# Loads of the modulations' weights during the recurrence: issued by ScalarE on its own DMA queue instead of by SyncE on the common one

## The chip, the core and the metric

The kernel runs on one core of a Trainium2 chip. The metric is the device time of one execution in microseconds (us), lower is better. The engines are TensorE (PE in the profile; its weight loads are PEld), VectorE (DVE), ScalarE (ACT), GpSimd (POOL) and SyncE (SP), which only issues DMA transfers. SPq stands for SP's own instruction sequence.

## What is computed

Two layers of a diffusion backbone over 512 latent tokens (l) and 256 context tokens (c), width 1024, all in float32. Cut to what matters here:

```
def ada_mod(cond, w, b):                 # nine modulations of 1024 columns for each layer
    m = jax.nn.silu(cond) @ w + b        # w: 1024 x 9216
    return m.reshape(cond.shape[:-1] + (N_MOD, D_MODEL))

for li in range(DEPTH):                  # DEPTH = 2
    ml, mc = ada_mod(c, mod_w[li], mod_b[li]), ada_mod(c_ctx, mod_w[li], mod_b[li])
    xl, xc = first SwiGLU half-step (modulations 0 to 2)
    out = concat(fourier(f), window_attention(q, k, v), rwkv7(r, k, v, ...)) @ w_out   # modulations 3 to 5
    xl, xc = second SwiGLU half-step (modulations 6 to 8)
```

The RWKV-7 part is a bidirectional recurrence over the tokens with a 64x64 state for each of six heads.

## The kernel before, in words

The work runs layer by layer: feed-forward half, input projections of the mixer, the recurrence (`rwkv`), output projection, feed-forward half. Python code emits the instructions; a scheduler then sets the order on each engine from its own estimate of when operands are ready. Each engine, and SP too, then works through its own sequence strictly in order: an instruction that waits for a semaphore holds up everything behind it on that engine.

**The recurrence** is done in six groups of 256 tokens in each layer (two directions, three blocks of tokens), with products over chunks of 64 tokens. Group numbers run from 0 to 5; `d_0_4` in the rows of the order is the DRAM scratch of layer 0, group 4.

**`inverses` (lines 930 to 998)** inverts, for a group, the small triangles on the diagonal. It is the part that goes through DRAM, and it matters below. Its steps: products on PE, copied out by ACT (L961, tile LAB); masked on DVE (L969, L971); written to DRAM (L975, `d<-W`); read back in another layout (L976, `W<-d`); 62 short DVE instructions that do the elimination (L987 and L989, thirty-one pairs, of which the first L987 has the form 96x31); written to DRAM again (L992), read back (L993); put on the diagonal (L997). DVE stands still at its first L987 until L976 has landed, whatever else is behind it.

**Fill work.** Attention (L1083 to L1140), the modulations that are needed later (`mod_steps`, L239) and part of the output projection (`out_part`) are pumped into the recurrence (`pump`), a piece for each stretch of PE work. `mod_steps` makes modulations 5 to 8 of the layer and, in layer 0, also 0 to 4 of the next one. Half a modulation takes two loads of weights, each 128 x 4 x 512 (1 MB), into two buffers (`wmod`, L251), eight matmuls for each load (L256, tile `pf`, one PSUM buffer), a copy by ACT (L262, tile `macc`), a 2 KB load of the bias into it (L263), short matmuls (L266 or L271), and a copy of the result (L267 or L272). A load has to wait until PE has used the buffer's last content.

The line that the change touches, and its surroundings:

```
def part(q, cs=cs, st=st):
    w = wp.tile([128, 4, 512], F32, name="wmod", bufs=2)
    self.dma(w, self.a["mod_w"][l, q * 512:(q + 1) * 512, cs].rearrange("(k p) c -> p k c", p=128))   # L251
    if q == 0:
        st["ps"] = pf([128, 512])
    for g in range(4):
        r = slice(32 * g, 32 * g + 32)
        self.behind(nc.tensor.matmul(st["ps"][r], lhsT=self.cTz[:, 4 * q + g], rhs=w[:, g], ...))     # L256
```

`self.dma` is `nc.sync.dma_start`: before the change all transfers of the kernel are issued by SP, on one queue. Other loads that SP issues in the recurrence: the groups' operands (`AtB`, `BtB`, `KI` in L1285, `HB` in L1287, `W<-opd` in L954), the queries of a token tile (`q<-qd`, L1062), the values' rows (`Z`, L1321).

Of the kernel before, what the change touches and what calls it, by code (L numbers as in the profile page):

```python
# [32 lines left out]
# tiles of the feed-forward columns in the chunks after the first; buffers of gated products: raw (then low), high  # L33
# [5 lines left out]
class Halves:  # L39
    """Products of weights and tokens by Strassen's scheme (Winograd's form): the halves are of the  # L40
    inner dimension, of the tokens, and gates with values; 7 products of quarters instead of 8."""

    def __init__(self, net, n0, n):
        self.net, self.nc, self.w = net, net.nc, n // 2
        hi, lo = net.hT["h"], net.hT["o"]
        m = self.w
        q = lambda x, t, k: x[:, 4 * k:4 * k + 4, n0 + t * m:n0 + t * m + m]
        self.a = {f"a{t + 1}{k + 1}": (q(hi, t, k), q(lo, t, k)) for t in range(2) for k in range(2)}
        # the quarter a21 isn't needed by itself
        self.a["s3"] = self.a["a21"]  # L50

    def sums(self, anchor):
        """The second half of the work comes behind the anchor."""
# [31 lines left out]
    def weights(self, wi, c0):  # L85
        """The quarters of a tile of gates and one of values, and their sums."""
        nc, net = self.nc, self.net
# [12 lines left out]
    def unit(self, ws, sg, pool):  # L100
        """silu(gates) * values."""
# [42 lines left out]
# buffers of the ring of weights that stay through the mixers' projections, and more: raw, split  # L144
# [3 lines left out]
class Net:  # L148
# [78 lines left out]
    def behind(self, inst, anchor=None):  # L227
        """The engine of both issues inst after the anchor."""
# [10 lines left out]
    def mod_steps(self, l, m, wp, pf):  # L239
        """Steps for the modulation m of layer l: the sums by quarters of the array, then their sums with the bias."""  # L240
# [3 lines left out]
        for h in range(2):  # L244
# [3 lines left out]
            def part(q, cs=cs, st=st):  # L248
                self.mark('mod')
                w = wp.tile([128, 4, 512], F32, name="wmod", bufs=2)  # L250
                self.dma(w, self.a["mod_w"][l, q * 512:(q + 1) * 512, cs].rearrange("(k p) c -> p k c", p=128))  # L251
# [24 lines left out]
    def mod(self, l, ms, stg, rows):  # L276
        """The modulations ms (at most two) of layer l."""
# [34 lines left out]
    def norm_cols(self, l, n, m_shift, m_scale):  # L312
        """Columns of g*(1+scale) and of shift, by stream."""
# [8 lines left out]
    def gate_row(self, l, n, m, s, half):  # L322
        """The row half*m*g, on all partitions."""
# [11 lines left out]
    # The arena's tiles hold rows in turn (4), loaded rows (2), halves of transposes (2) and gate rows (2);  # L335
    # in the feed-forward halves the sums of quarters of the normed tokens
# [18 lines left out]
    # In the passage from one part to the next the engines keep to the order of the program  # L355
# [10 lines left out]
    def squares(self, x, junk):  # L366
        """The root of the mean of the squares."""
# [18 lines left out]
    def prenorm(self, t, x, cols, xn, junk):  # L386
        """Normalises the token tile t; every second one is transposed with the one before it. Two steps."""
# [11 lines left out]
    def flush(self, rest=True):  # L399
        """Emits the transposes that were put off, behind products that needn't wait for them."""  # L400
        for e in self.late:
            e[0] -= 1
        while self.late and (rest or self.late[0][0] == 0):
            self.some(4)
            self.late.pop(0)[1]()
        if rest:
            self.some(4)

    def some(self, n=1):
        """What follows the transposes, by quarters."""  # L410
# [39 lines left out]
    def residual(self, t, o, grow, xn, po):  # L450
        """x + norm(o)*grow for the token tile t, with o's halves as they come. Three steps."""
# [3 lines left out]
        for i in range(2):  # L455
            cs = slice(i * 512, i * 512 + 512)
            # of the halves' mean squares
# [11 lines left out]
    def passage(self, toks, outs, post):  # L469
        """The last products of the tokens, by halves (outs), and what follows them, a token behind."""  # L470
# [27 lines left out]
    def load_w(self, srcs, shape):  # L498
        """Loads weights (pieces by columns, or by rows of two dimensions)."""
# [11 lines left out]
    def turning(self, j, name, shape, dt):  # L511
        """The next tile of the ring, raw (0) or split (1)."""
# [9 lines left out]
    def cut(self, x, e=None):  # L522
        """Splits x, of at most 512 columns in all, exactly: (high, low), each of float32r."""
# [9 lines left out]
    def split_w(self, srcs, shape, e=(None, None)):  # L533
        """Weights, split exactly, by halves of their first free dimension."""
# [4 lines left out]
    def prod(self, ps, w, s, c0, n):  # L539
        """Sums in ps the products of the weights w with n tokens of stream s, from c0."""  # L540
# [13 lines left out]
    def ffn(self, l, wi, wo, toks, post, last, mods=(), early=None):  # L554
        """last: loads that follow the last chunk's products with the tokens."""
# [10 lines left out]
        # the last 64 columns come first: gates and values in one tile  # L566
# [12 lines left out]
        def split_g(sg, w):  # L579
            gh = fp.tile([128, NT], F32R, name="gh", bufs=GB)  # L580
            if w == 64:
                # the low parts below the high ones
# [10 lines left out]
        def gated(sg, cs, w, pg, pu):  # L593
            """silu(gates) * values; of a tile with both, on its upper half."""
# [9 lines left out]
        def first(ch):  # L604
            """The first chunk, by pairs of token tiles, as they become ready."""
# [81 lines left out]
    def early_keys(self, l, raw):  # L687
        """The context's keys of the recurrence, while the latent tokens are on their way."""
# [10 lines left out]
    def mixer(self, l, need_ctx):  # L699
# [5 lines left out]
        with self.pool("mixo", bufs=1) as mo, ExitStack() as outer:  # L705
# [8 lines left out]
            # partial output projections: of the Fourier heads, and of the attention heads as well  # L714
            self.part = [[self.dp.tile([128, D], F32, name=f"part{l}_{j}_{i}") for i in range(6)] for j in range(2)]
            # decays over the chunks
            pcs = mo.tile([128, 2, 3, 12], F32, name="pcs")
            self.rw = dict(pcs=pcs)
            # in DRAM: head sums times values; values in token-major; queries; by direction the recurrence's
            # unit keys by the decay so far, rates and keys by its inverse, receptances by the decay  # L720
# [6 lines left out]
            # keys' high parts, on both halves, by head; low parts  # L727
# [5 lines left out]
            with self.pool("inp", side="right") as rp, ExitStack() as inner:  # L733
# [5 lines left out]
                def load(c0):  # L739
                    """Columns c0 (a list of pieces) of the input projection's weights, split."""  # L740
                    return self.split_w([win[:, :, c:c + w] for c, w in (c0 if isinstance(c0, list) else [(c0, 128)])], [128, 8, 128])

                def proj(c0, ctxs=True, pcx=None):
                    """Columns c0 of the input projection: (latent, context) in PSUM."""
# [9 lines left out]
                # the recurrence's inputs; the context's first, while the latent tokens are on their way  # L754
                self.mark('inp')
                # rows 96 to 101: the heads' rows scaled by k_k
# [65 lines left out]
                # row 64: ones, and the decays' bias  # L822
# [23 lines left out]
                def operands(z):  # L846
                    """The recurrence's operands of direction z."""
# [11 lines left out]
                    for p in range(3):  # L859
# [11 lines left out]
                        # av: twice the in-context rate, less one  # L871
# [26 lines left out]
                for p in range(3):  # L898
                    r = rs[p]
                    v = conv(6 + p, kns[p], True)  # L900
                    # values, token-major
# [9 lines left out]
                    # the heads' sums of products of keys and receptances, times the values  # L911
# [10 lines left out]
    def diagonals(self, pool):  # L922
        """The recurrence's operands of two heads, on the blocks of a diagonal; KI: keys beside it, identities on it."""
# [13 lines left out]
    def triangles(self, pool):  # L937
        """Buffers of the inverses of the recurrence's triangles."""
# [4 lines left out]
    def inverses(self, gi, z, t0, psum, mm):  # L943
        """Of a group of 256 tokens from t0, direction z, the products of rates and unit keys, and the inverses of
        their 32x32 blocks on the diagonal."""
# [18 lines left out]
        # the blocks on the diagonal, of every unit a row of blocks; their inverses  # L964
# [7 lines left out]
        # of every block on one partition the even columns of the inverse, on another the odd ones  # L972
# [803 lines left out]
```

## Time and profile before

| | us |
|---|---|
| median of three runs | 3571.68 (3569.08 to 3574.14) |
| span of the profiled execution | 3573.4 |
| recurrence of layer 0, with the fill work | about 890 to 1340 |
| recurrence of layer 1, the part with loads of `wmod` | about 2710 to 2930 |
| busy over the span: PE, DVE, ACT, POOL | 3262.0, 2352.3, 1378.0, 809.4 |
| loads of `wmod` (L251) | 52, of 1 MB each |

The page gives the span of the profiled execution from its first to its last instruction and no other time of it. The span lies inside the spread of the three runs and 1.7 us above their median, so terms that are summed against it are brought to the median by taking 1.7 us off. A matmul counts as busy from its start to a modelled end; at the lower of TensorE's two clock levels the same matmul shows about twice the duration. "Releaser" is what ended a wait.

### The profile page before, as it was taken

The page shows a single profiled execution, that of the slowest core. Times are in us where ns is not written, and L with a number is a line of the kernel's source. Part 1 is how long each engine was busy: PE and PEld are TensorE (multiplying, and loading weights), DVE is VectorE, ACT ScalarE, POOL GpSimd, SP SyncE. Part 2 cuts the span into 40 slices and gives each one's busy share as a digit, 9 for nine tenths or more (in the row PEclk, how much of TensorE's full clock was granted, in tenths as well). Part 3 has the DMA queues.
Part 4 walks back from the last instruction along what each step waited for, and adds up shares of the span by engine and source line. Part 5 has one row for each costly group of instructions (what it writes and reads, how often), then busy time and mean ns, then how long its engine had stood idle before and what let it go on. Part 6 is the DMA issues. An engine that isn't in the chain of part 4 may idle for free. (4 is left out here: it accounts for less than half of the span.)

```text
span 3573.4 us, 51830 instructions
## 1 busy us (share of the span) xinstructions
PE 3262.0 (91%) x19801; PEld 2729.5 (76%) x19801; DVE 2352.3 (66%) x4374; ACT 1378.0 (39%) x2818; POOL 809.4 (23%) x609
## 2 busy tenths in 40 slices
PE   7999998998778897999998999998995898979998
PEld 5689997776556655899997899997774676758997
DVE  4577777456466656677777767777464666467897
ACT  3333335342334334433335433335342433344444
POOL 0222222023101013322222322222041000024333
PEclk9999999999889988999999999999997878779999
DMA  5432224245667556222224222224355563253333
GB/s 179 148 119 71 71 69 138 87 141 134 153 172 177 160 187 214 60 69 68 71 71 140 61 71 65 71 71 138 97 166 119 157 157 71 68 182 89 101 107 101
DMA packets 540346, 410.13 MB, mean 115 GB/s; under 512 B 210405, under 2 KB 462188, under 8 KB 540098
## 3 DMA queue, kind: packets, MB, share of 16 engines
q1 hardware_dynamic: 540098, 406.82, 39.4%
q8 instruction: 156, 2.56, 0.3%
q14 instruction: 92, 0.75, 0.1%
HBM read 345.60 MB, written 61.16 MB: 114 GB/s over the span
## 5 line engine op out<-in xcount | busy, mean ns | idle before, releaser
L666 PE MATMUL po<-wq,gh 128*128 128x512 f32 (+1 forms) x1936 | 692.4, 408 | 43.6 <-ACT po L458 23.8
L529 ACT CAST wq<-raw 128x512 fp32r<-128x512 f32 (+1 forms) x626 | 383.7, 619 | 619.0 <-PE pq L112 438.8
L112 PE MATMUL pq<-hh,wq 128*128 128x384 f32 (+1 forms) x2432 | 612.8, 324 | 5.1 <-DVE st L132 2.1
L530 DVE TENSOR_TENSOR wq<-raw,wq 128x512 fp32r<-128x512 f32 x616 | 510.5, 838 | 102.3 <-ACT wq L529 97.0
L112 PE MATMUL pq<-arena,wq 128*128 128x384 f32 (+1 forms) x2736 | 491.5, 324 | 1.7 <-ACT st L116 1.1
L666 PEld LDWEIGHTS po<-wq,gh 128*128 128x128 f32 (+1 forms) x1936 | 368.6, 191 | 152.6 <-ACT po L458 31.0
L112 PEld LDWEIGHTS pq<-arena,wq 128*128 128x128 f32 x2736 | 451.3, 189 | 24.1 <-issue 4.3
L112 PEld LDWEIGHTS pq<-hh,wq 128*128 128x128 f32 x2432 | 431.6, 188 | 19.5 <-issue 5.7
L112 PE MATMUL pq<-ho,wq 128*128 128x384 f32 (+1 forms) x1216 | 394.1, 324 | 0.0
L666 PE MATMUL po<-wq,go 128*128 128x512 f32 x924 | 371.0, 402 | 2.6 <-DVE go L590 2.6
L529 ACT CAST wq<-t 128x512 fp32r<-128x512 f32 x228 | 140.7, 621 | 340.6 <-PE pq L112 303.2
L93 POOL TENSOR_TENSOR t<-raw 128x512 f32<-128x512 f32 x76 | 103.6, 1363 | 735.8 <-DVE wq L530 358.6
L672 DVE TENSOR_TENSOR accl<-accl,po 128x512 f32<-128x512 f32 x288 | 196.8, 684 | 100.8 <-PE po L666 99.0
L112 PEld LDWEIGHTS pq<-ho,wq 128*128 128x128 f32 x1216 | 229.3, 189 | 7.1 <-issue 0.9
L544 PE MATMUL pil<-hh,wq 128*128 128x512 f32 (+1 forms) x704 | 217.0, 387 | 7.9 <-DVE hh L432 5.6
L666 PEld LDWEIGHTS po<-wq,go 128*128 128x128 f32 x924 | 177.1, 192 | 32.5 <-DVE go L590 5.7
L530 DVE TENSOR_TENSOR wq<-t,wq 128x512 fp32r<-128x512 f32 x228 | 176.4, 779 | 28.3 <-ACT wq L529 23.5
L544 PE MATMUL pc<-hh,wq 128*128 128x256 f32 x976 | 179.1, 284 | 6.4 <-DVE hh L432 5.1
L97 POOL TENSOR_TENSOR t<-raw,t 128x512 f32<-128x512 f32 x76 | 117.1, 1540 | 283.2 <-DVE wq L530 283.1
L987 DVE TENSOR_TENSOR W<-W 96x126 f32<-96x126 f32 (+22 forms) x372 | 101.8, 275 | 113.1 <-DMA W<-d 106.1
L544 PEld LDWEIGHTS pil<-hh,wq 128*128 128x128 f32 x704 | 133.1, 200 | 39.1 <-DVE hh L432 6.0
L544 PEld LDWEIGHTS pc<-hh,wq 128*128 128x128 f32 x976 | 152.6, 191 | 7.6 <-DVE hh L432 5.9
(386 smaller groups left out, 5670.6 us busy)
## 6 DMA issues: line engine op xcount, KB each, us to landing
raw<-in_ffn_wi_dram SPq DMA_DIRECT2D x168, 512.0 KB
wmod<-in_mod_w_dram SPq DMA_DIRECT2D x52, 1024.0 KB
raw<-in_ffn_wo_dram SPq DMA_DIRECT2D x84, 512.0 KB
raw<-in_mix_w_in_dram SPq DMA_DIRECT2D x38, 512.0 KB
raw<-in_mod_w_dram SPq DMA_DIRECT2D x24, 512.0 KB
x_l<-arena SPq DMA_DIRECT2D x20, 512.0 KB
arena<-x_l SPq DMA_DIRECT2D x20, 512.0 KB
W<-opd SPq DMA_DIRECT2D x24, 384.0 KB
```

The lines of the kernel that those rows point to most:

```text
L93: e.tensor_sub(t1, b12, b11)
L97: e.tensor_sub(t4, b21, t2)
L112: net.last_mm = nc.tensor.matmul(ps[:, :m], lhsT=w[x][:, k], rhs=a[y][:, k], start=(j == 0), stop=(j == 11))
L529: nc.scalar.copy(q[:, 0], x)
L530: (e or nc.vector).tensor_sub(q[:, 1], x, r32(q[:, 0]))
L544: inst = self.nc.tensor.matmul(ps[:, :n], lhsT=w[kt // 4][wp][:, kt % 4], rhs=self.hT[s, hp][:, kt, c0:c0 + n], start=(j == 0), stop=(j == ...
L666: mm = nc.tensor.matmul(ps, lhsT=x[r, t0:t0 + 128], rhs=w[hf][y][r], start=(j == 0), stop=(j == len(todo) - 1))
L672: self.pin(nc.vector.tensor_add(acc[t][:, cs], acc[t][:, cs], ps))
L987: e.tensor_mul(tv, LB[:, i, ro][:, :, None].to_broadcast([96, n, w]), XB[:, i, co][:, None, :].to_broadcast([96, n, w]))
```

## The change

```diff
                 self.mark('mod')
                 w = wp.tile([128, 4, 512], F32, name="wmod", bufs=2)
-                self.dma(w, self.a["mod_w"][l, q * 512:(q + 1) * 512, cs].rearrange("(k p) c -> p k c", p=128))
+                nc.scalar.dma_start(w, self.a["mod_w"][l, q * 512:(q + 1) * 512, cs].rearrange("(k p) c -> p k c", p=128))
                 if q == 0:
```

The rest of the diff takes out comments and docstrings and changes no statement. The 52 loads leave SP's sequence and stand in ACT's. Because the scheduler sets the order anew, the instructions of both recurrences change places on every engine.

SP in the recurrence of layer 0, from the first DRAM write of group 4's inverses (L975) to the read behind it (L976); before:

```order
L975 DMA d_0_4_10200<-W_6655 128x12x32
L954 DMA W_7429<-opd_5305 128x3x256
L268 DMA md_8_110<-macc 2x512
L1062 DMA q<-qd_5304 128x6x128
L992 DMA d_0_3_9352<-W_7429 1536x1x16 x2
L251 DMA wmod<-in_mod_w_dram 128x4x512
L976 DMA W_6655<-d_0_4_10200 96x1x1024
```

and now:

```order
L975 DMA d_0_4_10200<-W_6655 128x12x32
L993 DMA W_7429<-d_0_3_9352 128x12x32
L954 DMA W_7429<-opd_5305 128x3x256
L268 DMA md_8_110<-macc 2x512
L976 DMA W_6655<-d_0_4_10200 96x1x1024
```

The queries' load (L1062), the writes of group 3 (L992) and a load of `wmod` no longer stand between the two steps of group 4.

SP a little later, the same two steps for group 5; before:

```order
L977 DMA W_7429<-in_eye_dram 96x512
L1321 DMA Z<-vtd_5303 64x12x64 x2
L975 DMA d_0_5_10724<-W_7429 128x12x32
L993 DMA W_6655<-d_0_4_10266 128x12x32
L976 DMA W_7429<-d_0_5_10724 96x1x1024
```

and now:

```order
L977 DMA W_7429<-in_eye_dram 96x512
L975 DMA d_0_5_10724<-W_7429 128x12x32
L1062 DMA q<-qd_5304 128x6x128
L993 DMA W_6655<-d_0_4_10266 128x12x32
L976 DMA W_7429<-d_0_5_10724 96x1x1024
```

Here a load of queries has moved in between them.

ACT around one copy of the modulations' products (L262) in layer 0; L1115 and L1130 belong to attention, L1377 and L1304 to the recurrence. Before:

```order
L1115 ACTIVATE pr<-pr,den 128x512
L262 COPY macc<-pf 128x512
L1130 COPY ptb<-at 128x512
L1377 COPY Z<-pz 64x3x64
L1304 COPY HB<-pa 128x4x64
```

and now, at a copy of the same kind:

```order
L251 DMA wmod<-in_mod_w_dram 128x4x512
L1115 ACTIVATE pr<-pr,den 128x512
L251 DMA wmod<-in_mod_w_dram 128x4x512
L262 COPY macc<-pf 128x512
L1130 COPY ptb<-at 128x512
L1313 COPY HB<-pa 64x4x64
L1377 COPY Z<-pz 64x3x64
```

The two loads for the next half of a modulation stand beside the copy, and ACT's copies for attention and the recurrence are queued behind them.

On VectorE the change moves the first L987 of a group against the mask before it (L971). Instructions that stand between the two, group by group: in layer 0, groups 1 to 5, 22, 52, 27, 34 and 16 before, and 17, 52, 10, 24 and 22 now; in layer 1, 14, 32, 20, 27 and 14 before, and 13, 35, 31, 19 and 17 now.

## Rows read from the trace of the kernel before

**Rows 1.** Issues of the loads in question, part 6 of the page

```profile
wmod<-in_mod_w_dram SPq DMA_DIRECT2D x52, 1024.0 KB
```

**Rows 2.** Busy time by stretch: PE, PEld, DVE, ACT, POOL, clock, DMA share, GB/s

```profile
890.00:1340.00 450.00, 373.35 (x3257) 266.18 (x3258) 262.57 (x802) 181.06 (x463) 40.02 (x39) 0.88 0.64 170
2710.00:2930.00 220.00, 177.44 (x1435) 129.64 (x1435) 119.83 (x406) 79.43 (x205) 18.77 (x18) 0.78 0.64 157
```

**Rows 3.** Waits, 890 to 1340, then 2680 to 3100: us in total, times, longest

```profile
DVE W L987 <- DMA W<-d: 57.6, 5, 17.2
DVE W L987 <- DMA W<-d: 41.2, 5, 10.2
```

**Rows 4.** The same, of SP's own sequence, for the same two stretches

```profile
SPq L251 <- PE pf L256: 49.0, 21, 12.9
SPq L251 <- PE pf L256: 37.0, 8, 11.7
```

**Rows 5.** PE in order of time: start, us, instructions [idle before, releaser]

```profile
946.89 1.02 PE L266 MATMUL pf<-macc,sel 128*2 128x512 f32 x2
...
961.44 0.91 PE L1261 MATMUL pz<-Z,HB 128*64 128x64 f32 x12 [8.10 <-DVE Z L1378]
...
1004.35 3.64 PE L256 MATMUL pf<-wmod,cTz 128*32 128x512 f32 x16 [6.66 <-ACT mcol L272]
...
1058.38 0.48 PE L1261 MATMUL pz<-Z,MG 128*64 128x64 f32 x2 [8.72 <-DVE MG L1352]
...
1123.19 0.47 PE L1261 MATMUL pz<-Z,MG 128*64 128x64 f32 x2 [13.74 <-DVE MG L1352]
...
1176.85 2.07 PE L1261 MATMUL pb<-HB 64*128 64x128 f32 x8 [8.48 <-DVE HB L1352]
...
2781.85 1.87 PE L266 MATMUL pf<-macc,sel 128*2 128x512 f32 x2 [7.95 <-DMA macc<-in_mod_b_dram]
```

**Rows 6.** SP in order of time, layer 0: start, us of issuing, transfer

```profile
906.98 10.70 SPq L1285 DMA_DIRECT2D AtB<-opd  x2
...
928.01 8.85 SPq L251 DMA_DIRECT2D wmod<-in_mod_w_dram  x2
...
937.84 0.39 SPq L975 DMA_DIRECT2D d<-W  x1
947.43 0.67 SPq L976 DMA_DIRECT2D W<-d  x1
...
1089.48 0.37 SPq L975 DMA_DIRECT2D d<-W  x1
...
1094.70 0.54 SPq L1062 DMA_DIRECT2D q<-qd  x1
1095.35 10.78 SPq L992 DMA_DIRECT2D d<-W  x2
...
1107.20 0.74 SPq L976 DMA_DIRECT2D W<-d  x1
...
1164.65 1.23 SPq L251 DMA_DIRECT2D wmod<-in_mod_w_dram  x2
```

**Rows 7.** SP in order of time, layer 1

```profile
2763.84 8.38 SPq L251 DMA_DIRECT2D wmod<-in_mod_w_dram  x2
...
2773.07 0.27 SPq L263 DMA_DIRECT2D macc<-in_mod_b_dram  x1
...
2814.67 0.37 SPq L975 DMA_DIRECT2D d<-W  x1
2821.34 0.67 SPq L976 DMA_DIRECT2D W<-d  x1
...
2843.98 7.87 SPq L1285 DMA_DIRECT2D AtB<-opd  x2
...
2995.91 0.37 SPq L975 DMA_DIRECT2D d<-W  x1
2998.64 0.70 SPq L976 DMA_DIRECT2D W<-d  x1
```

## The prediction

> **What bounds the kernel now.** I first read the busy times by stretch. The loads that move, 52 of 1 MB [rows 1], all lie in the two recurrences, and there PE is not full: in layer 0 it is busy for 373.35 of 450 us, in layer 1 for 177.44 of 220 us, at a mean granted clock of 0.88 and 0.78 of full speed [rows 2]. Idle PE time is 76.7 and 42.6 us, 119.3 in all. The share of the clock that was missing, 0.12 of 450 and 0.22 of 220 us, is another 54.0 and 48.4 us, 102.4 in all. So in these stretches each microsecond of idle PE went along with 102.4 / 119.3 = 0.86 us lost at the lower of the two levels (1.2 GHz), which follows the gaps; one microsecond of gap won or lost is priced at 1.86 us below.
>
> Next I looked for who makes the gaps. PE in order of time shows five large ones in layer 0 that lie on the same spots: 8.10, 6.66, 8.72, 13.74 and 8.48 us, 45.7 in all [rows 5]. The releasers named are results of DVE, or an ACT copy that itself stood behind one. The waits say what DVE was doing: at its first elimination step (L987) it stood for 57.6 us in five waits, until the read back from DRAM (`W<-d`) had landed, and for 41.2 us in five waits in layer 1 [rows 3]. So a DVE wait there reaches PE with 45.7 / 57.6 = 0.79 of its length.
>
> Last I read SP in order of time, because both legs of that trip through DRAM are issued there. The loads of `wmod` hold up SP in two ways: it stands at them until PE has freed the buffer, 49.0 us in 21 waits and 37.0 us in 8 [rows 4], and when the write to DRAM (`d<-W`) comes right behind a pair of loads, 2 MB lie ahead of it on the one queue. From the issue of the write to that of the read, which waits for the write, it took 947.43 - 937.84 = 9.6 us in the first such case [rows 6] and 2821.34 - 2814.67 = 6.7 us in the last of five [rows 7]. Late in layer 1, with no load of `wmod` left, it took 2998.64 - 2995.91 = 2.7 us [rows 7].
>
> **The change, part by part.** *Write legs.* Five legs of (9.6 + 6.7) / 2 = 8.1 us against 2.7 us would save 5 x 5.4 = 27 us of DVE waiting if the loads on the other queue no longer stood in the way, and nothing if they slow the small write as much from there. The DMA share is 0.64 in both stretches [rows 2], so engines are neither free nor full; I take the middle, 13.5 us, and keep 0 and 27 as ends.
>
> *Group 4 and group 5.* In group 4 the read was issued 17.7 us after the write, 10.78 us of which SP spent on one pair of small writes that it had to issue right behind a load of queries [rows 6]. The new order has no such load between the two steps of group 4, but puts one between those of group 5. I let +10.8 and -10.8 us cancel.
>
> *Cover.* The scheduler expects shorter trips now and places the first L987 earlier. Over the nine groups where DVE waited (layer 1's group 3 did not), 29 instructions fewer stand in front of it. One takes 262.57 / 802 = 0.33 us [rows 2], so 9.6 us of cover are given back. Net of the three: 3.9 us less DVE waiting, x 0.79 = 3.1 us of PE gaps.
>
> *Bias rows.* In layer 1 a 2 KB load of a bias, issued at 2773.07 right behind a pair of `wmod` loads [rows 7], kept PE idle for 7.95 us [rows 5]. On a queue without the pair it should land sooner: between 0 and 7.95 us, I take 4.0. With it goes the lower clock behind the gap (the same two matmuls took 1.87 us there and 1.02 us elsewhere [rows 5]); that is in the 0.86.
>
> *SP's own time.* A pair of loads takes SP 1.23 us to issue [rows 6], 26 pairs 32 us, and 86 us of standing at them. I cost this freedom at nothing beyond the legs above: the other loads in SP's sequence name no PE gap that would go.
>
> *ACT.* No row shows a DMA issued by ACT. If it costs what it costs SP, 26 pairs take 32 us of an engine that is busy for 181.06 of 450 us [rows 2]. Below, nothing reaches PE; above, all 32 us do. A gain is excluded, since ACT loses nothing else. I take 2 us, near the lower end: in the rows on PE the one gap that ACT ended [rows 5] was DVE's, so ACT has room. The wait for the buffer costs ACT nothing new in most places, because the load stands beside L262, which waits for matmuls of the same group.
>
> *Sum.* Gaps: -3.1 - 4.0 + 2.0 = -5.1 us, x 1.86 = -9.5 us. 3573.4 - 9.5 - 1.7 = 3562 us. With the ends of the legs and of the bias row on the good side the gaps shrink by 13.7 + 8.0 - 2.0 = 19.7 us, 37 us in all: 3535 us. A measurement of this kernel can tell about 0.2%, 7 us, from no change: below 3564.5 is faster, above 3578.8 slower.
>
> **The rivals.** *Nothing is left of it.* The legs shorten by a third only (9 us), the cover takes 9.6, the bias row gives 2 and ACT takes 2. That is about zero: 3573 us, 3565 to 3578. For it: the scheduler's earlier L987 is certain, the shorter leg is not. Against it: the 2.7 us of the clean leg.
>
> *The legs do not shorten at all.* What a queue of its own does for the small write rests on how the DMA engines take turns, which no row of before shows, as it has one queue only. If the loads slow it as before, the cover is lost for nothing: (7.6 + 2.0) x 1.86 = 17.9 us, 3590 us. The Trainium skill states this rule, against the change: in its page DMA: Bandwidth & Descriptors, section Issuing engines are not separate DMA queues, transfers from several issuing engines run on the same 16 DMA engines and interleave, and only the sequencer's issue time is saved. By that rule the first term would be 0 and the sum 3590 us; the trace of before speaks against its last half, since a write that shared the engines with no pair was 5.4 us faster per leg, but does not show two queues.
>
> *ACT is held where SP was held.* This one ends slower. SP's issues behind a load of queries or a long read take some 8 to 11 us. I count eleven of them where `wmod` is loaded (890 to 1283 and 2710 to 2930, 613 us), the first of 10.70 us at 906.98 [rows 6], the last of 7.87 us at 2843.98 [rows 7], about 100 us in all. If ACT's issue has to wait while SP's is stuck, 26 x 100 / 613 = 4.2 pairs meet it, with half of it, 4.6 us, left on average: 20 us of a standing ACT, with attention's and the recurrence's copies behind it. Should half reach PE, the sum is (10.0 - 7.1) x 1.86 = +5.4, 3577 us; should all, +24, 3596 us; I put it at 3585. It decides from two meetings on, where 7.1 us of gaps are eaten up. A load that ACT issues late, behind its own wait for DVE, adds to the same side. Against it: nothing shows that a queue that takes no more from SP takes no more from ACT. The Trainium skill's page Perfetto Trace Analysis, section DMA Instruction — HWDGE (DVE, Sync), has it that the block which generates descriptors is shared and locked by one sequencer at a time; by that the meetings would be real, and the sum up to 3596 us.
>
> **How the numbers follow.** Forecast, 3562 us: 0.42. Nothing left, 3573: 0.28. ACT held, 3585: 0.20. Legs as long as before, 3590: 0.10. Faster by over 0.2% is the first case, 0.42; within 0.2% the second, 0.28; slower the last two, 0.30. The first case reaches from 3535 to 3564, of which I leave out the end below 3543; the last two end at 3596 and 3590, and I cut at 3592. The first case's own range is 3543 to 3564.
>
> **What would show it.** Right: DVE's waits at L987 for `W<-d` fall from 98.8 us in all to some 95, with single ones shorter although less stands in front of them; legs behind a pair near 5 us; the gap at the bias row halved; PE's idle time in both stretches down by about 5 us and the clock up from 0.88 and 0.78. Wrong: ACT's issues of `wmod` of several us each, or PE gaps that end at an ACT copy queued behind such an issue, or matmuls on `wmod` that wait for the load; or legs still at 7 to 10 us.

## The result, and the profile after

| | before | after |
|---|---|---|
| median of eight runs each, us | 3572.91 (3568.43 to 3583.81) | 3605.19 (3584.57 to 3617.64) |
| ratio after to before, 95% interval | | 1.0082 (1.0059 to 1.0105) |
| time and span of the profiled execution, us | span 3573.4 | 3606.18, span 3604.4 |

The change makes the kernel slower by 0.82%, about 30 us. The forecast was 3562 us, the upper end of its range 3592 us: both missed.

First the loads themselves. The rows of L251 in both traces (duration min/median/max in ns, first and last start), the one before on SP:

```profile
L251 SPq DMA_DIRECT2D wmod<-in_mod_w_dram x52: 363/394/7593, 890.3 to 2907.1; - x52
```

and after, on ACT:

```profile
L251 ACTq DMA_DIRECT2D wmod<-in_mod_w_dram x52: 374/374/1170, 885.7 to 2961.0; - x52
```

So the move happened, and no issue on ACT took more than 1.17 us: what the third rival feared is not there.

Then the busy time by stretch, as in [rows 2], but with the bounds put at the same places of both programs: from the first transposes of L906 in a layer to the first matmul of L424 behind the output projection, and the passage between the two recurrences. Before:

```profile
869.50:1398.60 529.10, 432.42 (x3504) 309.42 (x3505) 306.11 (x892) 205.19 (x516) 65.30 (x63) 0.89 0.66 176
1398.60:2710.00 1311.40, 1257.91 (x6693) 1120.80 (x6692) 918.83 (x1354) 516.20 (x948) 350.18 (x250) 0.98 0.29 89
2710.00:3194.30 484.30, 402.93 (x2965) 299.28 (x2966) 267.92 (x803) 170.37 (x430) 54.29 (x53) 0.79 0.51 131
```

After:

```profile
869.00:1444.20 575.20, 478.91 (x3504) 342.61 (x3505) 306.96 (x892) 205.97 (x516) 63.11 (x63) 0.81 0.59 161
1444.20:2757.20 1313.00, 1260.02 (x6692) 1121.84 (x6690) 918.14 (x1354) 515.65 (x948) 350.51 (x250) 0.98 0.30 89
2757.20:3227.10 469.90, 375.31 (x2965) 280.96 (x2966) 269.67 (x803) 171.16 (x430) 54.21 (x53) 0.83 0.53 135
```

The same 3504 matmuls of layer 0 take 575.2 instead of 529.1 us. Length minus busy time of PE is its idle time: 96.7 us before, 96.3 after. In this pair of profiles all 46 us are in PE's busy time, 432.4 against 478.9, and the granted clock fell from 0.89 to 0.81. Layer 1 goes the other way: idle from 81.4 to 94.6, busy from 402.9 to 375.3, 14.4 us shorter. The passage between them is the same. The loss is in layer 0.

One caution on single profiles: two of the experiments below run the instructions of layer 0 in exactly the order and on the queue of before, and their profiles show 550.1 and 539.1 us for that stretch against 529.1, at busy times of 456.9 and 451.6 us. A third runs layer 0 exactly as in the changed kernel and shows 570.9 us, 464.2 of them busy and 106.7 idle. So a difference of some 20 us between two single profiles of layer 0 says nothing, and the profile of before is the shortest of its kind. Verdicts below rest on the medians; what is busy and what is idle time is read from all profiles of an order together.

DVE's waits for the two reads back from DRAM, as in [rows 3] (L987 waits for the first, L997 for the second), before in the two recurrences:

```profile
DVE DX L997 <- DMA W<-d: 4.5, 2, 3.1
DVE DX L997 <- DMA W<-d: 29.3, 1, 29.3
```

and after, layer 0, then layer 1 ("issue" is a wait for which the trace names no releaser):

```profile
DVE W L987 <- DMA W<-d: 28.2, 4, 8.3
DVE DX L997 <- DMA W<-d: 20.7, 4, 15.3
DVE W L987 <- issue: 13.3, 1, 13.3
DVE W L987 <- DMA W<-d: 48.0, 5, 17.1
DVE DX L997 <- DMA W<-d: 39.6, 3, 28.0
DVE W L987 <- issue: 15.3, 1, 15.3
```

At L987 DVE waits 28.2 + 13.3 = 41.5 us in layer 0 (57.6 before) but 63.3 in layer 1 (41.2 before); at L997 60.3 us in all, 33.8 before.

SP's own waits in layer 0 after, as in [rows 4]:

```profile
SPq L263 <- ACT macc L262: 71.1, 14, 20.4
SPq L1140 <- ACT ob L1138: 24.6, 3, 23.0
```

SP no longer stands at `wmod`, but at the bias row (L263), whose target ACT has to copy first.

### The profile page after: what moved, and what is told of

It reads as the page before. It is cut to its first block, busy times and chain, and to the rows that moved or that the text cites. A ratio compares the mean times of both kernels' runs of the same rounds, so it can differ in the third digit from the quotient of the medians.

```text
span 3604.4 us, 51818 instructions
## 1 busy us (share of the span) xinstructions
PE 3280.3 (91%) x19801; PEld 2743.2 (76%) x19801; DVE 2353.2 (65%) x4374; ACT 1378.8 (38%) x2818; POOL 806.0 (22%) x609
## 5 line engine op out<-in xcount | busy, mean ns | idle before, releaser
L987 DVE TENSOR_TENSOR W<-W 96x126 f32<-96x126 f32 (+22 forms) x372 | 102.3, 276 | 118.8 <-DMA W<-d 83.3
```

Of the source, the lines that this page charges most:

```text
L987: e.tensor_mul(tv, LB[:, i, ro][:, :, None].to_broadcast([96, n, w]), XB[:, i, co][:, None, :].to_broadcast([96, n, w]))
```

## The theories and the experiments

Three theories to begin with. **1:** SP is held at L263 instead, and what stands behind it comes late. **2:** the new order that the scheduler made costs, whatever the queue. **3:** the second queue costs, whatever the order. Others were formed on the way and stand in the expectations. To tell order from queue, a table of each engine's order can be taken from one of the two built programs and laid on a kernel; it adds no instruction and no wait between engines (`ORDER` lists each engine's instructions by their number; cut to its core):

```diff
-        Net(ctx, tc, args, out).run(stop)
+        Net(ctx, tc, args, out).run(stop); pinned(nc, tc)
+def pinned(nc, tc):
+    ins = list(nc.cur_bb.bb.instructions)
+    for e, seq in ORDER.items():
+        for a, b in zip(seq, seq[1:]):
+            tc.add_manual_dep(ins[b], ins[a].name, NoSync, reason="order of issue")
```

All ratios are to the kernel before on the same chip (medians of it 3575 to 3580 us), with 95% intervals.

### Order or queue

**Old order, loads on ACT** (the changed kernel, order of before on all engines).

> Every engine keeps the order that it had before the change; only the 52 loads of wmod leave SP's sequence and stand in ACT's, on ACT's queue, with no place prescribed. Theory 1 (SP is now held at the bias row L263, 71.1 us of SP's waits in layer 0 against 8.5, because the new order puts that row early): SP meets L263 late again, so at most 3573 us, perhaps 3560. Theory 2 (the new order as such costs, by where its gaps on PE fall and the clock with them): 3565 to 3580. Theory 3 (the second queue itself costs, in ACT's time or in the transfers that collide): about 3600.

Measured: 3591.1 us, 1.0038 (1.0018 to 1.0058). Between the values of theories 2 and 3: the queue alone costs some 14 us.

**New order, loads on SP** (the kernel before, order of the changed one).

> The reverse: every engine has the order that it has after the change, but the 52 loads of wmod are back in SP's sequence, on the common queue, with no place prescribed. Theory 1 (SP held at L263): SP stands at L263 as after the change and at wmod besides, so 3605 us or more. Theory 2 (the order as such): about 3605. Theory 3 (the second queue): about 3573.

Measured: 3599.8 us, 1.0062 (1.0044 to 1.0080). The order alone costs some 22 us. 0.38 + 0.62 = 1.00% against 0.82% (0.59 to 1.05) for both: within the intervals they add up.

**New order, bias rows on ACT too.**

```diff
-                self.dma(acc[2:3], self.a["mod_b"][l:l + 1, cs])
+                nc.scalar.dma_start(acc[2:3], self.a["mod_b"][l:l + 1, cs])
```

> The changed kernel with its order of every engine kept, but the 26 bias loads (L263) too are issued by ACT, behind the copy L262 that they wait for, so that SP never waits at them. Theory 1 (SP held at L263): the 71.1 us of SP's waits go, and the time comes back to 3580 us or below. Theory 2 (the order as such): within 8 us of 3605. Theory 3 (the second queue): 3605 or somewhat more, since more goes over ACT.

Measured: 3620.8 us, 1.0120 (1.0091 to 1.0149). SP's longest waits in layer 0 are now others:

```profile
SPq L1285 <- PE pa L1261: 91.0, 4, 37.7
SPq L1321 <- PE pz L1261: 32.9, 3, 22.5
```

The wait of 71.1 us is gone, SP now waits for PE to free the operands' buffers, and the kernel is no faster. Theory 1 falls: to free SP of this wait won nothing. The time also lies above the range of theory 2 (3597 to 3613 us), on the side of theory 3.

**Another order, loads on SP**, in the kernel before:

```diff
-PUMP0 = 10.0
+PUMP0 = 10.5
```

> The kernel before, loads on SP, with one number of the pump nudged: the first piece of fill work is due after 10.5 us of PE work instead of 10.0. It moves hardly any work, but the scheduler orders both recurrences anew, about as much as the change does (1508 rows of PE's order differ, 1938 of DVE's, 352 of SP's). Theory 2 (the order as such): the time differs from 3573 us by 7 us or more, to either side. Theories 1 and 3: within 7 us of 3573, unless the new order also puts the bias row early.

Measured: 3593.1 us, 1.0045 (1.0027 to 1.0062). An order drawn anew costs 16 us without any change of queue. Its layer 0 took 536.7 us, 455.6 of them busy and 81.1 idle. Against the one profile of before that is 15.6 us less idle and 23.2 us more busy time; against the two repeats of that order (451.6 and 456.9 us busy, 87.5 and 93.2 idle) the busy time is the same, and only the idle time is less.

### Which engine's order, where the loads start, and another load on the second queue

**PE in the old order, loads on ACT, the other engines left to the scheduler** (`ORDER` holds PE alone).

> Loads of wmod on ACT's queue as in the change, TensorE's order held as it was before the change; the scheduler sets the order of the other engines around it (1362 rows of DVE's order differ from before, 2294 from the changed kernel). Theory 2a (of the new order it is TensorE's own that costs, because it mixes short matmuls in so that the granted clock stays low while PE is busy): as with the whole old order on ACT's queue, 3583 to 3598 us. Theory 2b (the order of DVE, ACT and SP costs): 3600 us or more.

Measured: 3619.9 us, 1.0116 (1.0099 to 1.0132), on the side of 2b. Its layer 0:

```profile
868.80:1433.10 564.30, 454.62 (x3503) 330.72 (x3504) 307.56 (x892) 205.97 (x516) 63.84 (x63) 0.85 0.60 165
```

**PE in the new order, loads on SP, the others left to the scheduler** (PE alone again).

> Loads of wmod on SP as before, TensorE's order held as it is after the change; the scheduler sets the other engines' order around it. Theory 2a (TensorE's own order costs): 3592 to 3605 us, PE's busy time in layer 0 some 35 us longer than before at the same idle time. Theory 2b (the other engines' order): 3572 to 3582.

Measured: 3608.3 us, 1.0084 (1.0069 to 1.0100), 3 us above the range of 2a and far from that of 2b. Its layer 0:

```profile
871.00:1442.40 571.40, 468.73 (x3503) 333.62 (x3504) 304.12 (x892) 205.79 (x516) 63.30 (x63) 0.83 0.60 162
```

PE's new order is enough to lose, and PE's old order is not enough to avoid it. But the two runs lose in different ways, which shows when the profiles of both kernels and of all runs with a held order, those further below included, are sorted by PE's order, whatever the queue and the other engines' order:

| layer, PE's order | profiles | PE busy, us | PE idle, us | granted clock |
|---|---|---|---|---|
| 0, of before | 8 | 432 to 457 | 87 to 97, once 109.7 | 0.84 to 0.89 |
| 0, of the change | 5 | 464 to 479 | 93 to 107 | 0.81 to 0.83 |
| 1, of before | 7 | 400 to 415 | 73 to 84 | 0.77 to 0.79 |
| 1, of the change | 6 | 375 to 393 | 77 to 95 | 0.81 to 0.83 |

The busy times of the two orders do not overlap in either layer. PE's new order keeps PE busy for longer in layer 0, on the means by 24 us, and for less long in layer 1, by 26 us. The gain in layer 1 follows PE's order too (469.6 us in this run, 490.7 us in the run above). The idle time grows less clearly, on the means by 9 us in layer 0 (without the 109.7) and by 7 us in layer 1. The 109.7 us are those of the run above: with PE's old order and the other engines' new ones, PE's busy time (454.6 us) is that of the old order, and the loss is PE standing idle.

**Old order, loads on ACT at the old times** (a place for each load in ACT's table).

> Every engine in the order of before, loads of wmod on ACT's queue, but each put at that place of ACT's sequence that ACT had reached when SP issued the load in the profile of before; so the transfers start when they started before, on another queue. Theory 4 (with the old order the loads cost because on ACT they start earlier, as soon as the buffer is free, and take DMA time from the operands and the inverses' transfers that the recurrence waits for): 3568 to 3579 us. Theory 3 (the second queue itself, or ACT's time for the issues, costs wherever the loads stand): 3586 to 3595.

Measured: 3591.1 us, 1.0043 (1.0026 to 1.0060). Theory 4 falls, theory 3 stands: with the order kept and the starts nearly so, the second queue costs some 15 us. The traces show one wait that it adds. Before, SP issues the operands `HB` and 1.7 us later the first of two loads of `wmod`:

```profile
1073.08 1.59 SPq L1287 DMA_DIRECT2D HB<-opd  x1
1074.77 3.53 SPq L251 DMA_DIRECT2D wmod<-in_mod_w_dram  x2
```

ACT, which copies `HB` at L1293, finds it there:

```profile
1082.07 3.76 ACT L1293 COPY MG<-HB 64x512 f32<-64x512 f32 x6
```

In the run with the old order and the loads on ACT (the first experiment) the same three steps are

```profile
1065.58 1.38 SPq L1287 DMA_DIRECT2D HB<-opd  x1
```

```profile
1066.41 0.38 ACTq L251 DMA_DIRECT2D wmod<-in_mod_w_dram  x1
...
1068.12 0.37 ACTq L251 DMA_DIRECT2D wmod<-in_mod_w_dram  x1
...
1080.22 3.76 ACT L1293 COPY MG<-HB 64x512 f32<-64x512 f32 x6 [4.96 <-DMA HB<-opd]
```

14.6 us from issue to copy, the last 5.0 of them waiting, instead of at most 9.0. PE stood for 4.64 us behind ACT's next copy. In the run of this section the same copy came 13.9 us after the issue and waited for 5.4 us; in four more profiles with PE's order of before and the loads on SP it came after 8.3 to 9.1 us without a wait. The reading that fits: on one queue the operands went ahead of the loads that were issued after them, on two they share the engines with them. The Trainium skill (DMA: Bandwidth & Descriptors, section Issuing engines are not separate DMA queues) says that transfers of all issuing engines interleave on the same 16 DMA engines; this wait agrees. It is no account of the 15 us: layer 0 took 537.7 and 537.6 us in the two runs with the loads on ACT, within the 529 to 550 us of the profiles with the loads on SP.

**Queries on ACT, all else as before.**

```diff
-            self.dma(t, bass.AP(tensor=src.tensor, offset=src.offset, ap=[...]))   # L1062
+            nc.scalar.dma_start(t, bass.AP(tensor=src.tensor, offset=src.offset, ap=[...]))
```

> Every engine in the order of before, wmod on SP as before, but the ten loads of queries (L1062) issued by ACT instead. In layer 0 the two writes L992 behind such a load hold SP for 10.8 us before and for 18.4 us with the old order and wmod on ACT, and the read L976 of group 4 stands behind them. If the queries' load fills the queue and that is what holds SP, L992 falls to some 1.5 us, the 13.7 us wait of PE at L1352's result to about 5, and the time to 3550 to 3568 us. If the writes hold SP by themselves, or what the load takes from the DMA engines counts alone: 3570 to 3580.

Measured: 3585.4 us, 1.0028 (1.0014 to 1.0042). The hoped gain is not there, and the time lies above both ranges; even ten loads on a second queue cost 10 us. The trace gives the first theory its premise and not its result: the two writes L992 held SP for 2.72 us instead of 10.78, so it was the load of queries ahead of them that held it, but PE's wait at L1352's result was still 12.66 us (13.74 before).

### Layer by layer

The order of before up to the middle of the program and that of the changed kernel from there on, or the reverse; the queue is chosen by layer (`l and m > 4` holds in layer 1's recurrence alone).

**Layer 1 new, all loads on SP.**

> Every engine has the order of before through the recurrence of layer 0, and the changed kernel's order from the middle of the program on; all loads of wmod on SP. Theory 5 (the new order costs in layer 0, some 35 us there with the loads on SP, and gains some 14 us in layer 1; the two add): 3573 - 14, so 3553 to 3565 us. Theory 6 (any other order or timing than that of before costs 10 us and more; layer 1 looked better only because it came after a bad layer 0): 3575 to 3595.

Measured: 3569.5 us, 0.9980 (0.9961 to 0.9999). This is 4.5 us above the range of theory 5 and 5.5 below that of theory 6; a gain, if a small one, is nearer to theory 5.

**The change in layer 1 alone.**

```diff
-                self.dma(w, self.a["mod_w"][...])
+                (nc.scalar if l and m > 4 else nc.sync).dma_start(w, self.a["mod_w"][...])
```

> The change made in the recurrence of layer 1 alone: layer 0 in the order of before with its 36 loads on SP, then the changed kernel's order with its 16 loads on ACT at the places that they have there. Theory 5: as with all loads on SP or a few us more for the second queue, 3555 to 3569 us. Theory 6: 3575 to 3595.

Measured: 3566.1 us, 0.9970 (0.9952 to 0.9988). This beats both kernels, by 11 us the one before. With the loads on SP the same order gave 0.20%, so most of the gain goes with the order, and here the second queue cost nothing that can be seen. Its profile, layer 0 and layer 1:

```profile
871.10:1410.20 539.10, 451.55 (x3503) 323.89 (x3504) 305.43 (x892) 205.34 (x516) 64.49 (x63) 0.85 0.64 172
2723.40:3186.90 463.50, 376.76 (x2964) 281.46 (x2965) 268.90 (x800) 170.35 (x429) 52.87 (x53) 0.82 0.53 136
```

**The change in layer 0 alone** (the same line with the engines exchanged).

> The change made in the recurrence of layer 0 alone: the changed kernel's order there with 36 loads on ACT, then the order of before with 16 loads on SP. Theory 5: 3573 + 46, so 3610 to 3628 us. Theory 6 and the theory that the loss sits where ACT issues loads in either layer: 3590 to 3606.

Measured: 3627.2 us, 1.0136 (1.0110 to 1.0162). Theory 5 holds in both directions: some 49 us are lost in layer 0 and some 11 won back in layer 1, together 38, where the change measured 30, a difference within the intervals.

**Old order, each load one place later on SP.**

> The order of before on PE, DVE, ACT and POOL and all loads on SP, but each load of wmod stands one place later in SP's sequence than before (behind the transfer that followed it). One queue as before, a small disturbance of its times. If the 14 us of the two kernels with the old order and wmod on ACT come from the second queue (a load on ACT's queue shares the DMA engines with an operand load that was issued ahead of it, where one queue serves them in turn): 3568 to 3579 us. Theory 6 (any disturbance costs): 3583 to 3600.

Measured: 3602.0 us, 1.0072 (1.0049 to 1.0095), 2 us above the range of theory 6. One queue, old order on four engines, and still 26 us lost. It is no clean control, since many loads came to stand behind a bias row that waits for ACT. But it says that the 14 us of the second queue are no larger than what a small shift on the one queue does.

### Is it a draw of the scheduler's?

The edit is `PUMP0` alone, as above, in the changed kernel and in the one before; no order is held. **9.5 us, loads on ACT:**

> The changed kernel with the pump's first piece due after 9.5 us of PE work instead of 10.0, which makes the scheduler order both recurrences anew. Read beside its twin with the loads on SP. Theory 7 (what the change costs is a draw: each re-ordering gives a time of its own, some 3560 to 3620 us, and the queue adds at most about 8 us): ACT minus SP comes out of either sign over the three nudged pairs. Theory 8 (loads on ACT make the scheduler's order worse as a rule): ACT is 15 us or more slower than its twin in each pair.

**9.5 us, loads on SP:**

> Its twin: the kernel before with the first piece due after 9.5 us, loads on SP. Theory 7: 3560 to 3620 us, no nearer to 3573 than the kernel with the loads on ACT need be. Theory 8: below its twin by 15 us or more.

**11.0 us, loads on ACT:**

> The changed kernel with the first piece due after 11.0 us. Theory 7: 3560 to 3620 us, of either sign against its twin. Theory 8: 15 us or more above its twin.

**11.0 us, loads on SP:**

> Its twin with the loads on SP. Theory 7: 3560 to 3620 us. Theory 8: below its twin by 15 us or more.

**10.5 us, loads on ACT:**

> The changed kernel with the pump's first piece due after 10.5 us; its twin with the loads on SP ran before and took 3593 us, 1.0045 of the kernel before. The two pairs since gave +34 us (9.5) and +10 us (11.0) for ACT, the original pair +30. Theory 7 (a draw that may fall on either side): below 3593 us. Theory 8 (the order made with loads on ACT is slower as a rule): 3600 to 3630 us.

Measured: 3610.0, 3575.5, 3614.8, 3604.8 and 3607.7 us. As ratios to the kernel before:

| first piece due after | loads on SP | loads on ACT | difference |
|---|---|---|---|
| 9.5 us | 0.9998 (0.9981 to 1.0015) | 1.0098 (1.0076 to 1.0120) | 0.0100 |
| 10.0 us | 1 | 1.0082 (1.0059 to 1.0105) | 0.0082 |
| 10.5 us | 1.0045 (1.0027 to 1.0062) | 1.0084 (1.0064 to 1.0103) | 0.0039 |
| 11.0 us | 1.0082 (1.0057 to 1.0106) | 1.0108 (1.0083 to 1.0132) | 0.0026 |

Neither theory as it was put: the differences are all of one sign (against theory 7), though the last is not clear of zero, and two are below the 15 us of theory 8. What stands is between them. On SP a nudge that means nothing moves the time by up to 0.8%, and 10.0 was one of the two good draws; on ACT all four draws are near 1.009. On average over the four pairs the change costs 0.62%, 22 us; the rest of its 30 us comes from the draws at 10.0, where the one on SP beats the mean of its four by more (0.31%) than the one on ACT does (0.11%).

In layer 0 of these draws the loss is not busy time. PE was busy for 457.6, 445.8 and 453.4 us with the loads on ACT (9.5, 10.5 and 11.0), and for 463.3, 455.6 and 465.4 us with the loads on SP. It was idle for 104.3, 111.2 and 104.3 us on ACT, and for 85.8, 81.1 and 109.3 us on SP, the last in the slow draw. So what the section on the engines' orders finds of PE's busy time holds for the pair of orders at 10.0.

**Loads on GpSimd's queue**, against the changed kernel:

```diff
-                nc.scalar.dma_start(w, self.a["mod_w"][...])
+                nc.gpsimd.dma_start(w, self.a["mod_w"][...])
```

> The 52 loads of wmod on GpSimd's queue, neither on SP's nor on ACT's; the scheduler orders everything anew. Theory 9 (what makes the orders slow is that the loads leave SP's sequence and start when their buffer is free, wherever they go): 3595 to 3625 us. Theory 10 (it is that they stand between ACT's copies): 3565 to 3590 us, plus what GpSimd needs to issue them.

Measured: 3595.4 us, 1.0052 (1.0035 to 1.0069): at the foot of theory 9's range and 5 us above the end of theory 10's, without a price for GpSimd's issues. It doesn't separate the two. PE was idle for 108.1 us in layer 0, as in the draws with the loads on ACT.

## Why the prediction was wrong, point by point

**Write legs: the saving of 13.5 us did not come.** In the changed kernel the first leg has a pair of loads 4.6 and 3.6 us ahead of it, now on ACT's queue, and nothing else on SP between write and read:

```profile
929.33 0.38 ACTq L251 DMA_DIRECT2D wmod<-in_mod_w_dram  x1
930.25 0.37 ACTq L251 DMA_DIRECT2D wmod<-in_mod_w_dram  x1
```

```profile
933.89 0.39 SPq L975 DMA_DIRECT2D d<-W  x1
944.86 0.67 SPq L976 DMA_DIRECT2D W<-d  x1
```

That is 11.0 us where [rows 6] show 9.6, and where the same order with the loads on SP shows 8.5. Two other legs, with a load issued less than 1 us ahead, took 8.9 and 8.4 us. SP's waits at the read for the write in layer 0, before and after:

```profile
SPq L976 <- DMA d<-W: 15.7, 4, 9.1
SPq L976 <- DMA d<-W: 16.9, 3, 10.5
```

So the prediction's own sign of being wrong, "legs still at 7 to 10 us", was there. Legs do get short where the loads start at another time. In the run with the old order and the loads on ACT, the first leg is

```profile
940.28 0.40 SPq L975 DMA_DIRECT2D d<-W  x1
944.96 0.67 SPq L976 DMA_DIRECT2D W<-d  x1
```

4.7 us, but no load was issued in the 14 us ahead of it, while before one was issued 2.2 us ahead. DVE's waits at L987 in that run, in layer 0 and layer 1, were

```profile
DVE W L987 <- DMA W<-d: 46.3, 5, 21.6
DVE W L987 <- DMA W<-d: 31.9, 6, 9.5
```

78.2 us against 98.8. In the run with the loads on ACT at the old times they were 93.1 us, and two profiles that repeat layer 0 of before show 54.1 and 47.5 us there against 57.6. So what was saved came with other starts of the loads, and in part it is scatter.

**Group 4 and group 5: right; cover: undersized, and the second trip was left out.** The time from the write to the read fell from 17.7 to 8.5 us in group 4 and rose from 4.4 to 15.7 in group 5, so the two nearly cancelled. With the new order the wait at L987 is 104.8 us, not 95. The longest in layer 1 grew from 10.2 to 17.1 us. And what was late next was not asked: the second trip, through L992 and L993 to L997, where DVE's waits grew from 33.8 to 60.3 us. Three counts in the order (a load between two steps, 29 instructions) stood for a re-ordering of both recurrences on every engine.

**Bias row: wrong in its result.** The gap in layer 1 [rows 5] is still there, at the same length; PE after, in order of time:

```profile
2827.97 1.86 PE L266 MATMUL pf<-macc,sel 128*2 128x512 f32 x2 [7.83 <-DMA macc<-in_mod_b_dram]
```

The row did land sooner: the matmul started 4.4 us after the issue of the load (2823.60), before 8.8 us, which is the 4.0 that was taken. But SP came to that issue late, since it had stood for 12.15 us at the one ahead of it (L977, from 2811.40), where before it had stood for 8.38 us at the pair of loads [rows 7].

**SP's own time: right, by another way.** It was costed at nothing, and the run with the bias rows on ACT shows that a free SP was worth nothing there either. Nor did SP become as free as the issues of the loads suggest. In the old order with the loads on ACT it stood at the next issue on its own queue, where before it had stood for 8.85 us at the pair [rows 6]:

```profile
925.95 13.90 SPq L977 DMA_DIRECT2D W<-in_eye_dram  x1
```

**ACT: the row was read rightly, the path was missed.** 52 issues at a median of 0.374 us are 19 us of ACT's time, none above 1.17 us. But 2 us was the wrong term for the queue: with the order kept it costs 14 to 15 us, although DVE waited less at L987. The operands' wait above is one thing that it adds; where the rest lies was not shown.

**From DVE's waits to the time: the step that failed.** The sum let the time follow DVE's waits at L987, x 0.79 for what reaches PE and x 1.86 for the clock that follows the gaps, and it put nothing for PE's own new order. The changed kernel breaks this path in each layer. In layer 0 the waits at L987 fell by 16.1 us, PE's idle time stayed (96.7 and 96.3 us), and the layer took 46 us more. In layer 1 the waits rose by 22.1 us, the idle time by 13.2, and the layer took 14.4 us less. Over both layers the idle time rose by 12.8 us, and 1.86 times that, 24 us, comes near the measured 30; this is luck, as it fits neither layer. What the runs show in its place is the order. With the loads on SP it costs 22 us by itself, and PE's order sets how long the same matmuls keep PE busy: in layer 0 432 to 457 us in the old order and 464 to 479 in the new one, in layer 1 400 to 415 and 375 to 393.

The run with the old order and the loads on ACT also speaks against the price, if less clearly. PE's idle time in the two recurrences fell by 10.7 us (96.7 to 93.9 and 81.4 to 73.4), and its busy time rose by 11.4 + 12.1 us, of which the first is within the scatter of layer 0:

```profile
871.20:1408.90 537.70, 443.77 (x3504) 319.44 (x3505) 304.85 (x892) 205.03 (x516) 64.20 (x63) 0.86 0.63 173
2722.40:3210.80 488.40, 415.00 (x2965) 307.36 (x2966) 269.02 (x803) 170.77 (x431) 54.88 (x53) 0.77 0.51 130
```

Where part of the 46 us of layer 0 went can be seen in one stretch, from the products of `DX` and `NM` in the second group to the next long gap; before, then after:

```profile
1014.80:1049.70 34.90, 34.05 (x316) 26.77 (x316) 25.39 (x84) 15.97 (x42) 2.23 (x1) 0.95 0.66 160
```

```profile
1015.50:1064.30 48.80, 47.64 (x308) 34.49 (x308) 24.05 (x76) 15.73 (x37) 1.81 (x1) 0.66 0.67 153
```

About as many matmuls, hardly any idle time in either, 14 us more, at a granted clock of 0.66 instead of 0.95. The same matmuls took 46 to 51 us in all five profiles with PE's new order. With the old one they took 34 to 38 us in six of eight, but 42.4 and 48.1 us in the other two, so the old order too can fall to the lower level there. In the old order PE does the small products of the inverses there mostly in one run and the large ones in blocks of eight:

```profile
1018.99 1.03 PE L1261 MATMUL pa<-W 64*64 64x64 f32 x28
1019.95 1.16 PE L1261 MATMUL pb<-HB,DX 128*128 128x128 f32 x8
```

In the new one it takes many of them in turn, two by two, at the lower level (1.2 GHz; the granted clock from 1039 to 1049 is 0.50):

```profile
1040.38 0.47 PE L1261 MATMUL pa<-W 64*64 64x64 f32 x2
1040.79 0.79 PE L1261 MATMUL pb<-HB,QB 128*128 128x128 f32 x2
```

That the turns hold the clock down is argued, not shown: no run changed them alone. What is shown is that the order costs by itself, that it costs in layer 0 and gives back in layer 1, and that PE's own order moves its busy time both ways with the granted clock. The run with PE in the old order lost as much, but as idle time.

**The rivals.** "The legs do not shorten at all" was right on the legs behind a pair, and its 3590 us came nearest, 15 us short. The number is luck: it was made of lost cover at the price of 1.86 (and of the lost bias row: with the first term alone at 0 the sum is 3582 us), and order and queue made the loss. "Nothing is left" was 30 us off. "ACT is held where SP was held" had the sign and fell as a mechanism: in the old order on ACT, SP stood for 18.4 us in two issues,

```profile
1093.62 18.38 SPq L992 DMA_DIRECT2D d<-W  x2
```

the first of which alone took 15.78 us, and within that one ACT issued two loads:

```profile
1093.78 0.38 ACTq L251 DMA_DIRECT2D wmod<-in_mod_w_dram  x1
...
1096.12 0.37 ACTq L251 DMA_DIRECT2D wmod<-in_mod_w_dram  x1
```

No rival said "the scheduler makes another order, and this is worth tens of us by itself", although the prediction knew that every engine was re-ordered. That case could be priced beforehand: with the loads on SP, a nudge that means nothing moved the time by -0.02, 0.45 and 0.82%.

**Still open:** why four orders out of four are slow with the loads on ACT (the three nudged ones by idle time of PE in layer 0), where the 14 to 15 us of the second queue lie, which are no more than a small shift on the one queue cost, and what in PE's new order keeps the clock low in layer 0.

## What to carry to other kernels

Where a scheduler orders the program, moving one instruction is two changes; hold the order still to see what the move does by itself, and re-draw the order a few times to see what a draw is worth, before reading a gain or a loss out of the edit. Idle time of PE alone is no measure of a latency-bound stretch whose clock moves: compare length, idle and busy time between the same places of both programs, over several profiles of each order. Here a queue of its own for the big loads did not let a small write past the loads issued just ahead of it, and it let big ones in among the operands that were issued ahead of them.

## What the runs showed of the hardware that was not expected

- An issue in which SP stood for 15.78 us did not hold up ACT's issues in the same time (0.38 and 0.37 us).
- A 384 KB operand load, with two 1 MB loads issued 0.8 and 2.5 us after it on another queue, took 14.6 us until its reader could start, and 13.9 us with the loads 0.6 and 3.9 us after it. With the pair 1.7 us behind it on the same queue it took at most 9.0 us.
- A 192 KB write to DRAM with two 1 MB loads issued 4.6 and 3.6 us ahead of it on another queue was as slow (11.0 us until the read that waits for it) as one behind such loads on its own queue (9.6 us); with no load in the 14 us ahead it took 4.7 us.
- The same instructions in the same order on the same queue took 529, 539 and 550 us in layer 0 over three profiled executions, with PE busy for 432, 452 and 457 us and idle for 97, 88 and 93 us: the difference is busy time at a lower granted clock (0.89, 0.85 and 0.84).
